# Products with stationary weights: all wide matmuls of a weight tile, then all narrow ones

## The chip, the cores and the metric

The kernel runs on one core of one Trainium2 chip. The metric is the device time of one execution in microseconds.

## What is computed

The reference is a decoder trunk of two layers on 256 tokens of width 2048, in float32: a dilated sliding-window attention (layer A), a SwiGLU feed-forward, a multi-head latent attention (layer B), a second feed-forward, each with an RMS norm ahead and a residual sum behind, and a last norm. Nearly all work is products of the tokens with weight matrices:

```python
qkv = (xn @ w_qkv).reshape(b, s, N_A_GROUPS, 3, A_HEADS, A_HEAD_DIM)   # layer A: 3 groups of q, k, v
g, u = jnp.split(xn @ w_gu, 2, axis=-1)                                # feed-forward, hidden 5632
return (jax.nn.silu(g) * u) @ w_down
kv = (c @ w_kv_b).reshape(b, s, B_HEADS, B_NOPE_DIM + B_V_DIM)         # layer B
q = (cq @ w_q_b).reshape(b, s, B_HEADS, B_NOPE_DIM + B_ROPE_DIM)
```

## The kernel before

**Weights.** Every weight matrix is read once, in tiles of up to 1 MB in the order of use (`WeightStream`, from line 83). SP loads them ahead. Each float32 tile is split into two float32r parts, `hi` and `lo`, whose sum is the weight exactly: ScalarE (ACT) casts `hi` (L141), VectorE (DVE) subtracts to get `lo` (L142), in two halves per tile. Both parts have three buffers; the split runs two weight tiles ahead of TensorE (PE), so that the split of tile n + 2 writes the buffers of tile n - 1 and waits for PE's last use of each.

**Products.** The tokens' activations are split in the same way and lie side by side in one tile, `xT[:, k, 0:256]` (hi) and `xT[:, k, 256:512]` (lo). `product` (L423) fetches weight tile after weight tile and accumulates into one PSUM tile `acc` of two banks, of which there are two. It has two forms:

- `w_stationary` (L391): 128 columns of weights stand still, the tokens stream. For each of the 8 feature tiles `kk` of a weight tile and each of its 2 column groups `i`, there is a **wide** matmul of 512 columns (`hi` on tokens hi and lo, L398) and a **narrow** one of 256 columns (`lo` on tokens hi alone, L402), both into bank `i` of `acc`. They alternate: narrow, wide, narrow, wide, with the bank changed after each pair. Only at the first feature tile of a product the wide one comes first, since it starts the accumulation. It computes q and k of layer A (1536 pairs of a wide and a narrow), gate and up of both feed-forwards (2816 pairs), and in layer B keys, queries and their rotary parts (176 pairs, in weight tiles of 4 or 8 feature tiles and 1 or 2 column groups).
- `x_stationary` (L409): 128 tokens stand still and the weights stream, three matmuls per feature tile and token tile (L419, L420, L421), each with its own stationary tile, three in a row into the same bank. They are 512 columns wide; for the values of layer B 256.

Every matmul has its own weight load (LDWEIGHTS, the rows PEld).

**After a product.** `halves` adds the two halves of `acc`: ACT copies the second (L438), DVE adds the first (L439). Then follow, on DVE and ACT, rotary embedding and masks, or SiLU and the product of gate and up. `Later` puts the work that depends on these behind the matmuls of the following weight tiles: scores of layer A two weight tiles later, values three, in layer B one and two. A scheduler orders the instructions of every engine by its own estimate of when they are ready.

Of the kernel before, what the change touches and what calls it, by code (L numbers as in the profile page):

```python
# [16 lines left out]
P = 128  # L17
S = 256
NT = S // P
# [17 lines left out]
# Weight tiles between a head's projections and its scores, its values.  # L37
# [9 lines left out]
def shape_constants():  # L47
    """Identity, attention masks and rotary tables: functions of the shapes alone."""
    c = np.zeros((P, C_END), np.float32)
    c[:, C_ID:C_ID + P] = np.eye(P, dtype=np.float32)  # L50

    def allowed(q, k, window, dil):
        dist = q - k
        return (dist >= 0) & (dist <= window) & (dist % dil == 0)

    def put(at, blocks):
        m = np.concatenate([allowed(q[:, None], k[None, :], w, d) for q, k, w, d in blocks], axis=1)
        c[:, at:at + m.shape[1]] = np.where(m, np.float32(0.0), np.float32(NEG))

    # Layer A keeps the even tokens in tile 0 and the odd ones in tile 1.  # L60
    i = np.arange(P)
    par = (2 * i, 2 * i + 1)
    order = np.concatenate(par)
    put(C_M0, [(q, order, *A_GROUPS[0]) for q in par])
    put(C_M1, [(q, q, *A_GROUPS[1]) for q in par])
    put(C_M2, [(q, q, *A_GROUPS[2]) for q in par])
    put(C_MB, [(i, i, S, 1), (i + P, np.arange(S), S, 1)])

    def angles(dim):
        f = np.float32(THETA) ** (-np.arange(0, dim, 2, dtype=np.float32) / np.float32(dim))  # L70
        a = np.arange(S, dtype=np.float32)[:, None] * f.astype(np.float32)[None, :]
        return np.cos(a).T.astype(np.float32), np.sin(a).T.astype(np.float32)

    ca, sa = (t[:, order] for t in angles(A_ROT))
    c[:A_ROT, C_CA:C_CA + S] = np.concatenate([ca, ca], axis=0)
    c[:A_ROT, C_SA:C_SA + S] = np.concatenate([-sa, sa], axis=0)
    cb, sb = angles(ROPE)
    c[:, C_CB:C_CB + S] = np.concatenate([cb, cb, cb, cb], axis=0)
    c[:, C_SB:C_SB + S] = np.concatenate([-sb, sb, -sb, sb], axis=0)
    return c  # L80


class WeightStream:
    """Weight tiles in the order of use: loads run ahead, and each float32 tile is split
    exactly into two float32r parts (hi + lo) ahead of the matmuls. form: "dup" writes the
    columns of every k twice, "heads" puts the rotary columns of a pair of heads side by side."""
# [17 lines left out]
    def pieces(self, raw, hi, lo, form, gain):  # L104
        """(source, hi, lo, gain) of every split operation."""
        _, nk, ncol = raw.shape
        if form == "heads":
            for a, b, at in ((0, NOPE, 0), (NOPE, QH, 2 * NOPE)):
                src = raw.rearrange("p k (h e) -> p k h e", h=2)[:, :, :, a:b]
                dst = [t[:, :, at:at + 2 * (b - a)].rearrange("p k (h e) -> p k h e", h=2) for t in (hi, lo)]  # L110
                for hh in range(2):
                    yield src[:, :, hh, :], dst[0][:, :, hh, :], dst[1][:, :, hh, :], None
        elif gain is None:
            flat = lambda t: t.rearrange("p k c -> p (k c)")  # noqa: E731
            n = nk // 2
            for ks in (slice(0, n), slice(n, nk)):
                yield flat(raw[:, ks]), flat(hi[:, ks]), flat(lo[:, ks]), None
        else:
            for k in range(nk):
                src, dst = raw[:, k, :], [hi[:, k, :], lo[:, k, :]]  # L120
                if form == "dup":
                    src = src.unsqueeze(1).broadcast_to([P, 2, ncol])
                    dst = [t.rearrange("p (o c) -> p o c", o=2) for t in dst]
                yield src, dst[0], dst[1], gain[:, k:k + 1]

    def split(self, upto):
        nc = self.nc
        while self.n_split < min(upto, len(self.units)):
# [8 lines left out]
            view = lambda t: t[:, :nk * ncol].rearrange("p (k c) -> p k c", c=ncol)  # noqa: E731  # L137
# [23 lines left out]
class Later:  # L161
    """Work put behind the matmuls of the following weight tiles, so that TensorE has those to do
    while the other engines prepare its operands."""
# [16 lines left out]
def kernel(ctx, tc, consts, x, attn_norm_g, ffn_norm_g, a_w_qkv, a_w_o, kv_norm_g,  # L180
# [23 lines left out]
    # TensorE's clock rises after some microseconds of work: have it up when the data is here.  # L204
# [10 lines left out]
    def gain_cols(vec, name):  # L215
        """vec [n * P] -> [P, n]: rows of P, to be turned by a transpose."""
        n = vec.shape[0] // P
        row = tmp.tile([P, 2, S], F32, tag="t1", name=name + "_row")[:n, 0, :P]
        nc.scalar.dma_start(out=row, in_=vec.rearrange("(k p) -> k p", p=P))
        cols = cpool.tile([P, n], F32, name=name)  # L220

        def turn():
            ps = bank()
            nc.tensor.transpose(out=ps[:, :n], in_=row, identity=ident[:n, :n])
            nc.vector.tensor_copy(out=cols, in_=ps[:, :n])
        return cols, turn
# [9 lines left out]
    def load_rest():  # L236
        """The constants and gains that the first products don't need."""
# [78 lines left out]
    con = lambda at, n, rows=P: cst[:rows, at - P:at - P + n]  # noqa: E731  # L316
# [6 lines left out]
    def put_split(dst_hi, dst_lo, src, scale=None):  # L323
        """dst_hi + dst_lo = src (times a value per partition), exactly."""
# [8 lines left out]
    def squares(src, total, on_vector=False):  # L333
        """total [P, 1] = the sum of squares of src [P, n] along the free axis."""
# [9 lines left out]
    def transposed(srcs, dstT, k0, gain):  # L344
        """srcs: [P tokens, n] by token tile -> dstT[:, k0 + j, hi 0:S | lo S:2S], features on partitions."""
# [16 lines left out]
    def rsqrt_mean(ssq, n, dst):  # L362
        """dst = (ssq / n + eps) ** -0.5."""
# [4 lines left out]
    def token_scale(ssq, name):  # L368
        """rms scale by token from partial sums of squares [P, NT, n]."""
# [6 lines left out]
    def across(r, name):  # L376
        """r [P tokens, NT] -> [P, S], the tokens' values along the free axis of every partition."""
# [13 lines left out]
    def w_stationary(acc, hi, lo, xT, k0, first, last, cols):  # L391
        """acc[:, i, :] += (weights' columns cols(i))^T [xT hi | xT lo], lo parts of weights on xT hi."""
        nk = hi.shape[1]
        for kk in range(nk):
            k = k0 + kk
            for i, sl in enumerate(cols):
                st, sp = first and kk == 0, last and kk == nk - 1
                big_mm = lambda: mm(out=acc[:, i, :], lhsT=sl(hi, kk), rhs=xT[:, k, :],  # noqa: B023,E731  # L398
                                    start=st, stop=sp)  # noqa: B023
                if st:  # L400
                    big_mm()
                mm(out=acc[:, i, 0:S], lhsT=sl(lo, kk), rhs=xT[:, k, 0:S], start=False, stop=False)  # L402
                if not st:
                    big_mm()
# [4 lines left out]
    def x_stationary(acc, hi, lo, xT, k0, first, last, rhs=None, ncol=512, ts=range(NT)):  # L409
        """acc[:, t, :] += (tokens of tile t) @ weights."""  # L410
# [12 lines left out]
    def product(stationary, xT, K, **kw):  # L423
        """xT's K feature tiles with the next weight tiles, into a new accumulator."""
# [10 lines left out]
    def halves(acc, n, dst):  # L435
        """dst [P, n, S] = acc[:, :, :S] + acc[:, :, S:]."""
# [4 lines left out]
    def masked(dst, ps, mk, mx):  # L441
        """dst = ps + mk, mx = its maximum by row."""
# [3 lines left out]
    def softmax(parts, m, scale, nscale):  # L446
        """parts[t] [P queries, keys] masked scores, m [P, NT] their maxima -> probabilities."""
        nb = small.tile([P, NT], F32, tag="sm_nb", name="sm_nb")
        if isinstance(scale, float):
            nc.vector.tensor_scalar(out=nb, in0=m, scalar1=nscale, scalar2=None, op0=ALU.mult)  # L450
            by = lambda t: scale  # noqa: E731
        else:
            nc.vector.tensor_tensor(out=nb, in0=m, in1=nscale, op=ALU.mult)
            by = lambda t: scale[:, t:t + 1]  # noqa: E731
# [10 lines left out]
    def keys_first(blocks):  # L465
        """Transposes of [P, P] blocks of probabilities, side by side."""
# [27 lines left out]
    with tc.tile_pool(name="attn_a", bufs=2) as ap:  # L494

        def rope_a(t):
            sw = ap.tile([A_ROT, 2, S], F32, tag="sw", name="sw", bufs=1)
            nc.vector.stream_shuffle(sw, t[:A_ROT], swap)
            bc = lambda r: r.unsqueeze(1).broadcast_to([A_ROT, 2, S])  # noqa: E731
# [22 lines left out]
        def values_a(head, sm, vs):  # L522
# [11 lines left out]
            back = lambda d: d.rearrange("p (i t) -> p t i", t=NT)  # noqa: E731  # L534
# [38 lines left out]
    def out_projection(acc, oT, gain, name):  # L573
        """h += attention output @ w_o (its first columns in acc); the next normed operand,
        still to be scaled by token, and that scale."""
# [12 lines left out]
    def ffn(xT, rstd, finish):  # L588
        """h += swiglu(xT scaled by token); finish(c, t) when a piece of h is complete."""
        row = {}  # L590
        later.put(1, lambda: row.update(R=across(rstd, "R")))
        with tc.tile_pool(name="ffn", bufs=2) as fp:
            for part, (k0, n) in enumerate(FFN_PARTS):
# [15 lines left out]
                def add(acc, c, t):  # L609
                    nc.vector.scalar_tensor_tensor(out=chunk(t, c), in0=acc[:, t, :], scalar=rstd[:, t:t + 1],  # L610
                                                   in1=chunk(t, c), op0=ALU.mult, op1=ALU.add)
                    if last:  # noqa: B023
                        finish(c, t)

                for c in range(4):
# [4 lines left out]
                    else:  # the very last columns: one token tile after the other  # L620
# [29 lines left out]
    with tc.tile_pool(name="attn_b", bufs=2) as bp:  # L650

        def rope_b(dst, t):
            """dst(rows) = rotary of t [P = 2 x (32 | 32), S]."""
# [8 lines left out]
        def latent(at, gain, lag):  # L662
            """rms_norm(xT @ (gained weights)) into ccT, transposed and gained."""
# [25 lines left out]
        # Rotary queries of one head of a pair each, zero in the other head's rows.  # L689
# [127 lines left out]
```

## Time and profile before

| | |
|---|---|
| runs | 2730.53, 2730.87, 2733.0 us; median 2730.87 us |
| span of the profiled execution, first to last instruction | 2728.2 us, 2.7 us under that median |
| PE busy | 2715.6 us (100%) |
| DVE, ACT busy | 1612.6 us (59%), 1204.2 us (44%) |
| DMA | 495.91 MB, 182 GB/s on average |

The time of the profiled execution itself is not on the page; its span is. Busy PE means that some matmul is under way, not that matmuls start as fast as they can: matmuls are pipelined and the next one starts before the record of the one ahead ends. The distance between starts is to be read from the timeline.

### The profile page before, as it was taken

To read this page: it belongs to the slowest core of one execution; us is meant where nothing else is said; L and a number is where in the kernel's file an instruction comes from. 1 tells how busy PE (TensorE), PEld (TensorE's weight loads), DVE (VectorE), ACT (ScalarE), POOL (GpSimd) and SP (SyncE) were. 2 spreads that over 40 slices of the span, in tenths; PEclk is the share of its full clock that TensorE was granted. 3 is DMA by queue.
4 is the path that set the end of the run, shared out by engine and by line. 5 is a ranking of instruction groups with operands and counts; after the bars stand their busy time and mean duration, and the time that the engine had idled before them with its cause. 6 is when DMAs were issued, how large, how long until landed. Compare 5 with 4: busy or idle time off the path is not lost.

```text
span 2728.2 us, 34772 instructions
## 1 busy us (share of the span) xinstructions
PE 2715.6 (100%) x14398; PEld 2323.1 (85%) x14398; DVE 1612.6 (59%) x2240; ACT 1204.2 (44%) x1605; POOL 5.5 (0%) x12
## 2 busy tenths in 40 slices
PE   9999999999999999999999999999999999999998
PEld 7888888888888888888888888888888888888887
DVE  5666576576477555545555555587555555555554
ACT  5344444443434444434443444555444434443443
POOL 0000000000000000000000000000000000000000
PEclk9999999999999999999999999999999999999999
DMA  7545555554554555555555555454555555555553
GB/s 282 182 162 171 181 171 170 185 182 161 182 175 166 201 181 188 187 190 194 188 185 187 185 187 196 140 156 145 174 181 186 194 190 187 187 190 192 185 201 124
DMA packets 389870, 495.91 MB, mean 182 GB/s; under 512 B 9848, under 2 KB 293200, under 8 KB 389200
## 3 DMA queue, kind: packets, MB, share of 16 engines
q1 hardware_dynamic: 389088, 492.63, 54.2%
q8 instruction: 113, 1.85, 0.3%
q10 hardware_dynamic: 624, 1.07, 0.1%
q14 instruction: 45, 0.37, 0.0%
HBM read 491.57 MB, written 2.10 MB: 181 GB/s over the span
## 4 chain that ended last, share of the span: by engine, by line
PE 98%; DVE 0%; issue 0%; ACT 0%; DMA 0%; SPq 0%; POOL 0%; POOLq 0%; DVEq 0%; ACTq 0%
PE acc L398 39%; PE acc L402 20%; PE acc L420 12%; PE acc L421 12%; PE acc L419 12%; PE bank L513 1%; PE bank L470 1%; PE bank L528 1%; PE bank L351 1%; PE bank L532 1%; PE bank L705 0%; PE bank L704 0%; PE bank L715 0%; DMA xt<-in_x_dram 0%; DVE lo L142 0%
## 5 line engine op out<-in xcount | busy, mean ns | idle before, releaser
L142 DVE TENSOR_TENSOR lo<-raw,hi 128x1024 fp32r<-128x1024 f32 (+2 forms) x930 | 1082.4, 1193 | 570.4 <-ACT hi L141 570.1
L141 ACT CAST hi<-raw 128x1024 fp32r<-128x1024 f32 (+2 forms) x930 | 912.7, 1030 | 859.7 <-issue 358.8
L398 PE MATMUL acc<-xT_f,hi 128*128 128x512 f32 x2816 | 987.6, 398 | 0.0
L402 PE MATMUL acc<-xT_f,lo 128*128 128x256 f32 x2816 | 776.9, 281 | 0.0
L398 PEld LDWEIGHTS acc<-xT_f,hi 128*128 128x128 f32 x2816 | 523.8, 188 | 122.7
L398 PE MATMUL acc<-xT_a,hi 128*128 128x512 f32 x1536 | 544.2, 399 | 0.0
L402 PEld LDWEIGHTS acc<-xT_f,lo 128*128 128x128 f32 x2816 | 531.8, 189 | 7.8
L402 PE MATMUL acc<-xT_a,lo 128*128 128x256 f32 x1536 | 423.7, 281 | 0.0
L398 PEld LDWEIGHTS acc<-xT_a,hi 128*128 128x128 f32 x1536 | 286.8, 188 | 63.5
L438 ACT COPY t<-acc 128x512 f32<-128x512 f32 x161 | 92.7, 576 | 502.8 <-PE acc L398 502.8
L402 PEld LDWEIGHTS acc<-xT_a,lo 128*128 128x128 f32 x1536 | 289.5, 188 | 3.7
L419 PE MATMUL acc<-hi,hT 128*128 128x512 f32 x704 | 274.1, 389 | 0.0
L421 PE MATMUL acc<-hi,hT 128*128 128x512 f32 x704 | 273.9, 389 | 0.0
L420 PE MATMUL acc<-lo,hT 128*128 128x512 f32 x704 | 273.9, 389 | 0.0
L439 DVE TENSOR_TENSOR gu<-acc,t 128x512 f32<-128x512 f32 x88 | 60.9, 692 | 244.2 <-ACT t L438 244.2
L421 PEld LDWEIGHTS acc<-hi,hT 128*128 128x128 f32 x704 | 132.1, 188 | 27.5
L420 PEld LDWEIGHTS acc<-lo,hT 128*128 128x128 f32 x704 | 132.1, 188 | 27.3
L419 PEld LDWEIGHTS acc<-hi,hT 128*128 128x128 f32 x704 | 132.2, 188 | 27.2
L420 PE MATMUL acc<-lo,xT_a 128*128 128x512 f32 x384 | 150.3, 391 | 0.8 <-DVE lo L142 0.8
L421 PE MATMUL acc<-hi,xT_a 128*128 128x512 f32 x384 | 151.0, 393 | 0.0
L419 PE MATMUL acc<-hi,xT_a 128*128 128x512 f32 x384 | 150.9, 393 | 0.0
L420 PEld LDWEIGHTS acc<-lo,xT_a 128*128 128x128 f32 x384 | 72.3, 188 | 16.1 <-DVE lo L142 1.5
(169 smaller groups left out, 2080.7 us busy)
## 6 DMA issues: line engine op xcount, KB each, us to landing
raw<-in_ffn_w_gu_dram SPq DMA_DIRECT2D x176, 1024.0 KB, 4.9
raw<-in_a_w_qkv_dram SPq DMA_DIRECT2D x143, 1024.0 KB, 4.9
raw<-in_ffn_w_down_dram SPq DMA_DIRECT2D x88, 1024.0 KB, 4.9
raw<-in_a_w_o_dram SPq DMA_DIRECT2D x16, 1024.0 KB, 4.9
raw<-in_b_w_o_dram SPq DMA_DIRECT2D x16, 1024.0 KB, 4.9
raw<-in_b_w_kv_b_dram SPq DMA_DIRECT2D x8, 1024.0 KB, 5.4
raw<-in_b_w_q_b_dram SPq DMA_DIRECT2D x8, 768.0 KB, 4.6
raw<-in_b_w_q_a_dram SPq DMA_DIRECT2D x4, 1024.0 KB, 5.0
```

Source lines behind the costliest of these rows:

```text
L141: nc.scalar.copy(out=h, in_=src)
L142: nc.vector.tensor_tensor(out=l, in0=src, in1=h.bitcast(F32), op=ALU.subtract)
L351: nc.tensor.transpose(out=ps[:, jj * S + t * P:jj * S + (t + 1) * P], in_=srcs[t][:, (j + jj) * P:(j + jj + 1) * P], identity=ident)
L398: big_mm = lambda: mm(out=acc[:, i, :], lhsT=sl(hi, kk), rhs=xT[:, k, :], # noqa: B023,E731 start=st, stop=sp) # noqa: B023
L402: mm(out=acc[:, i, 0:S], lhsT=sl(lo, kk), rhs=xT[:, k, 0:S], start=False, stop=False)
L419: mm(out=acc[:, t, :ncol], lhsT=xh, rhs=rhs(hi, kk), start=st, stop=False)
L420: mm(out=acc[:, t, :ncol], lhsT=xh, rhs=rhs(lo, kk), start=False, stop=False)
L421: mm(out=acc[:, t, :ncol], lhsT=xl, rhs=rhs(hi, kk), start=False, stop=sp)
L438: nc.scalar.copy(out=t1[:, :n, :], in_=acc[:, :n, S:2 * S])
L439: nc.vector.tensor_tensor(out=dst, in0=acc[:, :n, 0:S], in1=t1[:, :n, :], op=ALU.add)
L470: nc.tensor.transpose(out=ps[:, i * P:(i + 1) * P], in_=b, identity=ident)
L513: mm(out=ps[:, t * n:(t + 1) * n], lhsT=q[:, hh, qt], rhs=kt[:, hh, ks], start=True, stop=True)
```

## The change

In `w_stationary` the loops are turned round: for each weight tile first all wide matmuls (column group by column group, the 8 feature tiles of one after each other), then all narrow ones in the same order. The matmuls, their operands and their number are the same. The accumulation still starts with a wide matmul, and it now ends with a narrow one. The rest of the change takes out comments.

```diff
     def w_stationary(acc, hi, lo, xT, k0, first, last, cols):
         nk = hi.shape[1]
-        for kk in range(nk):
-            k = k0 + kk
-            for i, sl in enumerate(cols):
-                st, sp = first and kk == 0, last and kk == nk - 1
-                big_mm = lambda: mm(out=acc[:, i, :], lhsT=sl(hi, kk), rhs=xT[:, k, :],
-                                    start=st, stop=sp)
-                if st:
-                    big_mm()
-                mm(out=acc[:, i, 0:S], lhsT=sl(lo, kk), rhs=xT[:, k, 0:S], start=False, stop=False)
-                if not st:
-                    big_mm()
+        for i, sl in enumerate(cols):
+            for kk in range(nk):
+                mm(out=acc[:, i, :], lhsT=sl(hi, kk), rhs=xT[:, k0 + kk, :], start=first and kk == 0, stop=False)
+        for i, sl in enumerate(cols):
+            for kk in range(nk):
+                mm(out=acc[:, i, 0:S], lhsT=sl(lo, kk), rhs=xT[:, k0 + kk, 0:S], start=False,
+                   stop=last and kk == nk - 1)
```

On PE, in the middle of the first feed-forward (`xT_f` are its tokens), over the end of one product and the start of the next, before:

```order
L402 MATMUL acc<-xT_f_7145,lo 128x256
L398 MATMUL acc<-xT_f_7145,hi 128x512
L402 MATMUL acc<-xT_f_7145,lo 128x256
L398 MATMUL acc<-xT_f_7145,hi 128x512 x2
L402 MATMUL acc<-xT_f_7145,lo 128x256
L398 MATMUL acc<-xT_f_7145,hi 128x512
L402 MATMUL acc<-xT_f_7145,lo 128x256 x2
L398 MATMUL acc<-xT_f_7145,hi 128x512
```

and after (the lines are three fewer, so L397 is the wide one and L400 the narrow one):

```order
L397 MATMUL acc<-xT_f_7145,hi 128x512 x16
L400 MATMUL acc<-xT_f_7145,lo 128x256 x16
L397 MATMUL acc<-xT_f_7145,hi 128x512 x16
L400 MATMUL acc<-xT_f_7145,lo 128x256 x16
L397 MATMUL acc<-xT_f_7145,hi 128x512 x16
```

A weight tile is now a run of 16 wide and a run of 16 narrow matmuls.

On ACT, in the same feed-forward (`t` is the copied half of an accumulator, `gu` gate and up, `hT` their product), before:

```order
L438 COPY t_8250<-acc 128x512
L141 CAST hi<-raw 128x1024 x2
L604 ACTIVATE gu_8249<-gu_8249 128x512
L141 CAST hi<-raw 128x1024 x2
L438 COPY t_8337<-acc 128x512
L141 CAST hi<-raw 128x1024 x2
L326 CAST hT<-gu_8336 128x2x256
```

and after:

```order
L435 COPY t_8250<-acc 128x512
L141 CAST hi<-raw 128x1024
L601 ACTIVATE gu_8249<-gu_8249 128x512
L141 CAST hi<-raw 128x1024 x3
L435 COPY t_8337<-acc 128x512
L141 CAST hi<-raw 128x1024
L326 CAST hT<-gu_8336 128x2x256
```

One cast of the coming weight tiles has moved ahead of each copy out of an accumulator, and one behind it is left. In layer B the same happens to the second copy of a pair of heads (the rotary queries), in six of the eight pairs; before and after:

```order
L438 COPY t_14260<-acc 128x512
L438 COPY t_14264<-acc 128x256
L141 CAST hi<-raw 128x1024 x2
L326 CAST oT_b<-bank 128x256
L472 COPY pt<-bank 128x384
```

```order
L435 COPY t_14260<-acc 128x512
L141 CAST hi<-raw 128x1024
L435 COPY t_14264<-acc 128x256
L141 CAST hi<-raw 128x1024
L326 CAST oT_b<-bank 128x256
```

The second copy stands behind one half of a cast. DVE's order in layer B is unchanged; in the feed-forward and in layer A a half of the `lo` split stands ahead of later steps of a product's chain.

## Rows read from the trace of the kernel before

**Rows 1.** The page: busy time, granted clock, chain, groups (busy us, mean ns).

```profile
PE 2715.6 (100%) x14398; PEld 2323.1 (85%) x14398; DVE 1612.6 (59%) x2240; ACT 1204.2 (44%) x1605; POOL 5.5 (0%) x12
...
PEclk9999999999999999999999999999999999999999
...
PE 98%; DVE 0%; issue 0%; ACT 0%; DMA 0%; SPq 0%; POOL 0%; POOLq 0%; DVEq 0%; ACTq 0%
PE acc L398 39%; PE acc L402 20%; PE acc L420 12%; PE acc L421 12%; PE acc L419 12%; PE bank L513 1%; PE bank L470 1%; PE bank L528 1%; PE bank L351 1%; PE bank L532 1%; PE bank L705 0%; PE bank L704 0%; PE bank L715 0%; DMA xt<-in_x_dram 0%; DVE lo L142 0%
...
L142 DVE TENSOR_TENSOR lo<-raw,hi 128x1024 fp32r<-128x1024 f32 (+2 forms) x930 | 1082.4, 1193 | 570.4 <-ACT hi L141 570.1
L141 ACT CAST hi<-raw 128x1024 fp32r<-128x1024 f32 (+2 forms) x930 | 912.7, 1030 | 859.7 <-issue 358.8
L398 PE MATMUL acc<-xT_f,hi 128*128 128x512 f32 x2816 | 987.6, 398 | 0.0
...
L398 PE MATMUL acc<-xT_a,hi 128*128 128x512 f32 x1536 | 544.2, 399 | 0.0
```

**Rows 2.** Windows, narrow line L402, feed-forward: window, length, PE busy (count), PEld, clock, DMA.

```profile
1248.83:1429.41 180.58, 141.18 (x512) 96.70 (x512) 1.00 0.57 187
```

**Rows 3.** Timeline, feed-forward, a border of products: start us, length us, engine, line.

```profile
1303.61 0.40 PE L398 MATMUL acc<-xT_f,hi 128*128 128x512 f32 x1
1303.85 0.28 PE L402 MATMUL acc<-xT_f,lo 128*128 128x256 f32 x1
1303.85 0.19 PEld L398 LDWEIGHTS acc<-xT_f,hi 128*128 128x128 f32 x1
1303.97 0.40 PE L398 MATMUL acc<-xT_f,hi 128*128 128x512 f32 x1
...
1304.67 0.40 PE L398 MATMUL acc<-xT_f,hi 128*128 128x512 f32 x1
...
1305.03 0.62 PE L398 MATMUL acc<-xT_f,hi 128*128 128x512 f32 x2
...
1305.46 0.59 ACT L438 COPY t<-acc 128x512 f32<-128x512 f32 x1 [3.61 <-PE acc L398]
1305.49 0.28 PE L402 MATMUL acc<-xT_f,lo 128*128 128x256 f32 x1
...
1305.84 0.40 PE L402 MATMUL acc<-xT_f,lo 128*128 128x256 f32 x2
...
1306.07 0.40 PE L398 MATMUL acc<-xT_f,hi 128*128 128x512 f32 x1
...
1306.08 0.69 DVE L439 TENSOR_TENSOR gu<-acc,t 128x512 f32<-128x512 f32 x1 [2.79 <-ACT t L438]
```

**Rows 4.** Timeline, PE, second product of the feed-forward: first and last of 99 rows.

```profile
1169.72 0.39 PE L421 MATMUL acc<-hi,hT 128*128 128x512 f32 x1
...
1191.94 0.39 PE L420 MATMUL acc<-lo,hT 128*128 128x512 f32 x1
```

**Rows 5.** Timeline, PE, values of layer B: first and last of 24 rows.

```profile
1775.93 0.28 PE L419 MATMUL acc<-hi,ccT 128*128 128x256 f32 x1
...
1778.69 0.28 PE L421 MATMUL acc<-hi,ccT 128*128 128x256 f32 x1
```

**Rows 6.** Windows, L402, uninterrupted stretches of layer A: first, third, last of 24, sum.

```profile
81.62:114.08 32.46, 25.50 (x92) 17.37 (x92) 1.00 0.55 182
...
141.08:161.54 20.46, 16.28 (x59) 11.11 (x59) 1.00 0.48 159
...
873.62:882.98 9.36, 7.48 (x27) 5.07 (x27) 1.00 0.39 126
sum 461.50, PE 364.68 PEld 248.69; mean PE 15.19 PEld 10.36
```

**Rows 7.** Window, layer B's heads, all engines: length, busy of PE, PEld, DVE, ACT.

```profile
1770.00:1890.00 120.00, 119.05 (x751) 106.47 (x750) 104.52 (x281) 73.24 (x168) 0.00 (x0) 1.00 0.46 145
```

**Rows 8.** PE's waits, the longest for an accumulator: total us, times, longest.

```profile
PE acc L398 <- ACT vb L731: 0.7, 1, 0.7
```

## The prediction

> **What bounds the kernel now.** I read the page first: TensorE (PE) is busy over the whole span, its granted clock is full in every slice, and the chain that ended last is 98% PE; 59% of it lies on the two lines that the change touches, L398 (wide) and L402 (narrow) [rows 1]. DVE and ACT, which make the weights' parts, are busy 59% and 44%. So the time is the number of matmuls times the distance from the start of one to the start of the next. The duration of a record is no use for that: a wide's record lasts 398 ns [rows 1], but the next matmul starts well before its end, as the timeline shows [rows 3]. I therefore took distances between starts from timelines and windows.
>
> In the feed-forward part, 512 narrows (and as many wides) fill 180.58 us [rows 2]: 352.7 ns per pair. The timeline shows its pattern: wide 1303.61, narrow 1303.85, wide 1303.97, and the wide three pairs after the first at 1304.67, so 1.06 us for three pairs [rows 3]; a wide takes about 236 ns to the next start and a narrow 117 ns. In layer A the same loop runs at more than one pace: 32.46 us for 92 pairs (352.8 ns), but 20.46 us for 59 (346.8 ns). All 24 uninterrupted stretches together, of which the first, the third, the last and the sum stand in the rows, hold 4 x 330 = 1320 pairs (the four groups of heads repeat one pattern of counts) in 461.50 us: 349.6 ns [rows 6].
>
> **What the new order costs, from the nearest rows.** No long run of wides or of narrows of this function is in the trace, but x_stationary has both, with a new stationary tile for every matmul as here.
> - Wide after wide: the first and the last of 99 rows of the feed-forward's second product start at 1169.72 and 1191.94 us [rows 4]: 22.22/98 = 226.7 ns. The function itself does it once, where one product ends and the next begins: two wides from 1305.03 to the narrow at 1305.49, 0.46 us [rows 3]; with 0.227 for the second, the one after a narrow keeps its 0.235.
> - Narrow after narrow: in layer B 24 narrow matmuls in a row start from 1775.93 to 1778.69 us [rows 5]: 2.76/23 = 120.0 ns. The function does it once per product: two narrows from 1305.84 to the wide at 1306.07, 0.23 us [rows 3], which leaves some 115 ns for the one behind a wide.
>
> So what counts is what stood ahead: a wide is 9 ns cheaper behind a wide, a narrow 5 ns dearer behind a narrow.
>
> A weight tile of 8 feature tiles and 2 column groups is now 16 wides, then 16 narrows: 235 + 15 x 226.7 + 115 + 15 x 120.0 = 5550 ns, or 346.9 per pair. That the fastest stretch of the alternating loop also runs at 346.8 [rows 6] suggests that this is the floor of both orders, which the alternation reaches only at times.
>
> **The sum.**
> - Feed-forward, 2816 pairs [rows 1]: 352.7 - 346.9 = 5.8 ns each, 16.3 us.
> - Layer A, 1536 pairs [rows 1]: 349.6 - 346.9 = 2.7 ns each, 4.1 us.
> - Layer B, 176 pairs, 4 to 8 at a time: at the same 2.7 ns 0.5 us. Against it stands a moved instruction: in six of eight pairs of heads half a cast of weights now stands ahead of ACT's second copy out of an accumulator. Such a cast takes 1.03 us on average [rows 1], so at most 6.2 us if all reached PE, and nothing if the next scores have that much slack. PE stands idle for 0.95 of 120 us there, with DVE at 87% [rows 7]. I take these two as cancelling: 0.
>
> Together 20.4 us off. The profiled execution's span is 2728.2 us; the median of the runs is 2730.9, with 2.7 us around the span. Off the median: **2710.5 us**.
>
> **Edits that I cost at nothing.** The instructions are the same in kind and number, the scores and values go to the same products, and PE still waits twice per weight tile for ACT's parts and twice for DVE's. The last wide now frees the hi tile some 1.9 us before the weight tile ends (16 x 0.12), so the cast two tiles ahead begins earlier and stands ahead of ACT's copy of the accumulator; two halves of 1.03 us [rows 1] end some 0.2 us after the product. On DVE a half of the next split (1.19 us [rows 1]) stands ahead of the addition that empties the accumulator, the rest of the product's chain behind it. Today the copy starts at 1305.46 us with the product's end and DVE's addition at 1306.08 [rows 3]; both would come 1 to 2 us later. The accumulator is wanted again one product later, some 11 us, which hides it; the scores of layer A run two weight tiles, 11 us, behind their product, and the wait for lo is looser than before, since lo is used last. If that cover went, PE would lose those 1 to 2 us per product. The longest wait of PE for an accumulator is 0.7 us today, and it comes once [rows 8].
>
> **Rivals.**
> 1. *The order does not matter: no change.* A wide costs 236 and a narrow 117 ns in this loop because of its operands (tokens stream, weights stand), whatever stands ahead. For it: the two kinds of loop differ in what streams, and the wide that follows a narrow at a border of products costs the same as within. Against: the second of two wides at that border comes out at 227, if the first keeps its 235, as in x_stationary. The sum is then 0: 2731 us. The Trainium skill has a rule to this effect (TensorE: Matmul & The Clock Gate, Back-to-back issue gap): an isolated matmul's distance is its columns divided by 2.4 GHz plus 2.5 ns, so 216 and 109 ns, 325 a pair in any order, and no gain here. The trace disagrees with its size: no order comes below 346 ns, and 120.0 in a run stands against 109.
> 2. *A run of narrows waits for its weights: slower.* A weight load is recorded with 0.19 us, more than a narrow's 120 ns [rows 3, 5], and with wides between, only every other load has so short a slot. If in this loop a load were shown in full, a narrow in a run would go to 188 ns: 4230 of them (15 of 16 on 272 weight tiles, 150 in layer B) x 68 = 288 us; halfway 144 us, so 2855 us. It costs more than the order brings from about 125 ns per narrow on, 5 ns above the rows. Against it: layer B's run of 24, with a load each, holds 120.0 ns throughout. The Trainium skill puts a load at its columns divided by 1.2 GHz, 107 ns for 128 (same page, LDWEIGHTS (loading the stationary operand)), as long as a narrow streams; by that the loads would fit, as that run shows.
> 3. *Half of the wides' gain is had.* Wides at 231 ns behind each other: 15 x 4.3 ns given back on each of 272 weight tiles, 17.5 us, so 2728 us. It counts with rival 1.
> 4. *Narrows stay at 115 ns behind each other:* 15 x 5 ns x 272 = 20.4 us more gain, 2690 us. The run in layer B is against it.
> 5. *The change does not do what it says.* The built order shows rows of 16 and 16, broken only by scores and values of layer A, so this I leave out.
>
> **How the numbers follow.** Chances: the forecast 0.82; rivals 1 and 3 together 0.10, of which 0.08 end within 0.2%; rival 2, 0.05; rival 4, 0.03. Within 0.2% is 5.5 us either way, about what a measurement of this kernel can tell from no change. The forecast itself reaches from 2702 (narrows in a run keep 2 of the 5 ns, 8 us) to 2723 (wides keep 1.6 ns of their 9, 6.5 us, and layer B's moved casts cost their 6 us). That leaves out rival 4 below and rivals 1 to 3 above, some 0.18. Faster: 0.82 + 0.03 + 0.02 = 0.87; same 0.08; slower 0.05.
>
> **What would show it.** In the profile after: the timeline of a weight tile with wides 0.227 us apart and narrows 0.120; the 512 pairs of the feed-forward window in some 177.6 us; layer A's stretches all at 347 ns; PE's idle in layer B near 1 us; the granted clock still full. Narrows of 125 ns and more mean rival 2, wides of 235 ns rival 1. Waits of PE for accumulators, or for scores' operands, would mean that the moved casts and copies reach it. The prediction is wrong if the distances depend on the operands and not on what stood ahead.

## The result and the profile after

The changed kernel takes 2714.7 us (median of five runs, 2713.9 to 2715.6) against 2731.5 us for the kernel before on the same chip (median of five, 2730.5 to 2733.0): a ratio of 0.9939, with a 95% interval from 0.9927 to 0.9951, 16.8 us off. Timed again beside the experiments it came to 2715.7 us against 2730.1, 0.9947 [0.9933, 0.9961]. So it is faster, by 0.6% where 0.75% was forecast: 4.2 us above the forecast of 2710.5 us, within the stated range of 2702 to 2723 us.

The page of the changed kernel, the lines that answer to [rows 1]. L397 is now the wide line and L400 the narrow one:

```profile
span 2713.6 us, 34687 instructions
...
PE 2698.9 (99%) x14398; PEld 2327.4 (86%) x14398; DVE 1607.1 (59%) x2240; ACT 1205.5 (44%) x1605; POOL 5.5 (0%) x12
...
PEclk9999999999999999999999999999999999999999
...
PE 98%; DVE 1%; ACT 0%; issue 0%; DMA 0%; SPq 0%; POOL 0%; POOLq 0%; DVEq 0%; ACTq 0%
...
L397 PE MATMUL acc<-xT_f,hi 128*128 128x512 f32 x2816 | 672.0, 391 | 0.0
...
L400 PE MATMUL acc<-xT_f,lo 128*128 128x256 f32 x2816 | 365.3, 283 | 0.0
```

PE still bounds the kernel, at full granted clock, with the same number of matmuls. The busy time of L397 has fallen by 316 us against L398 before, and that says nothing: a line's busy time counts every moment in which one of its records runs. Before, a wide and a narrow record overlapped and both lines counted that time; in a run, records of the same line overlap and it is counted once. The distances between starts tell what moved. First the window over the same 512 pairs as [rows 2], narrow line; then, on the timeline, the runs of 16 (start, length to the end of the last, count):

```profile
1244.82:1422.92 178.10, 66.25 (x512) 65.64 (x512) 1.00 0.58 191
```

```profile
1265.14 2.08 PE L400 MATMUL acc<-xT_f,lo 128*128 128x256 f32 x16
1267.06 3.82 PE L397 MATMUL acc<-xT_f,hi 128*128 128x512 f32 x16
1270.71 2.08 PE L400 MATMUL acc<-xT_f,lo 128*128 128x256 f32 x16
1272.62 1.55 PE L397 MATMUL acc<-xT_f,hi 128*128 128x512 f32 x6
```

178.10 us for 512 pairs is 347.9 ns a pair; it was 352.7. A run of 16 narrows takes 1.92 us from its first start to that of the next run, a run of 16 wides 3.65 us. That is 228 ns per wide, not 226.7, and the timeline shows which wides it is. This is the same run, cut behind its sixth wide:

```profile
1266.94 0.28 PE L400 MATMUL acc<-xT_f,lo 128*128 128x256 f32 x1
1267.06 1.55 PE L397 MATMUL acc<-xT_f,hi 128*128 128x512 f32 x6
```

The sixth ends 1.55 us behind the start of the first and is 0.39 us long, so it starts 1.16 us behind it: five distances of 232 ns. In the trace they are 233, 236, 228, 233 and 231 ns, to within a nanosecond the same five in every run of wides of the feed-forwards that stands behind narrows; from the sixth on all are 226 or 227, and the remaining eleven make up 2.49 of the 3.65 us. Behind x_stationary, whose matmuls are 512 columns wide too, there are no slow wides, in layer A and in the feed-forwards alike. Here is the first run of layer A:

```profile
81.17 0.39 PE L418 MATMUL acc<-hi,xT_a 128*128 128x512 f32 x1
81.39 3.79 PE L397 MATMUL acc<-xT_a,hi 128*128 128x512 f32 x16
85.02 2.08 PE L400 MATMUL acc<-xT_a,lo 128*128 128x256 f32 x16
```

From 81.39 to 85.02 are 3.63 us, 226.9 ns per wide.

Where the time went, by the start of each stage's first matmul on the two timelines (us):

| stage | before | after | off | forecast off |
|---|---|---|---|---|
| up to the first q, k product | 80.61 | 81.39 | -0.8 | 0 |
| layer A, from there to its output projection | 802.75 | 800.37 | 2.4 | 4.1 |
| first feed-forward | 740.00 | 733.29 | 6.7 | 8.15 |
| second feed-forward, to the end | 745.54 | 738.85 | 6.7 | 8.15 |
| layer B and both output projections | 359.33 | 359.67 | -0.3 | 0 |

That is 14.7 us between the two profiled spans; the medians, of five executions each, are 16.8 us apart. In the first line the second part of the tokens landed later in the profile after: PE's transposition of it starts at 8.79 us, not at 8.05. None of the matmuls that the change reorders stands ahead of it, and over all profiles of this case the line lies between 80.3 and 82.1 us.

### The profile page after: what moved, and what is told of

Read it like the earlier page. It is cut to its first block, busy times and chain, and to the rows that moved or that the text cites. A ratio compares the mean times of both kernels' runs of the same rounds, so it can differ in the third digit from the quotient of the medians.

```text
span 2713.6 us, 34687 instructions
## 1 busy us (share of the span) xinstructions
PE 2698.9 (99%) x14398; PEld 2327.4 (86%) x14398; DVE 1607.1 (59%) x2240; ACT 1205.5 (44%) x1605; POOL 5.5 (0%) x12
## 4 chain that ended last, share of the span: by engine, by line
PE 98%; DVE 1%; ACT 0%; issue 0%; DMA 0%; SPq 0%; POOL 0%; POOLq 0%; DVEq 0%; ACTq 0%
PE acc L397 38%; PE acc L400 20%; PE acc L417 12%; PE acc L418 12%; PE acc L416 12%; PE bank L510 1%; PE bank L467 1%; PE bank L525 1%; PE bank L351 1%; PE bank L529 1%; PE bank L702 0%; PE bank L701 0%; PE bank L712 0%; DVE lo L142 0%; DMA xt<-in_x_dram 0%
## 5 line engine op out<-in xcount | busy, mean ns | idle before, releaser
L397 PE MATMUL acc<-xT_f,hi 128*128 128x512 f32 x2816 | 672.0, 391 | 0.0
L397 PEld LDWEIGHTS acc<-xT_f,hi 128*128 128x128 f32 x2816 | 517.8, 188 | 100.8 <-DVE xT_f L330 0.3
L397 PE MATMUL acc<-xT_a,hi 128*128 128x512 f32 x1536 | 379.4, 395 | 0.0
L400 PEld LDWEIGHTS acc<-xT_f,lo 128*128 128x128 f32 x2816 | 361.0, 191 | 13.7
L400 PE MATMUL acc<-xT_f,lo 128*128 128x256 f32 x2816 | 365.3, 283 | 0.0
L397 PEld LDWEIGHTS acc<-xT_a,hi 128*128 128x128 f32 x1536 | 281.5, 188 | 53.9
L400 PEld LDWEIGHTS acc<-xT_a,lo 128*128 128x128 f32 x1536 | 196.9, 191 | 7.5
L400 PE MATMUL acc<-xT_a,lo 128*128 128x256 f32 x1536 | 199.2, 283 | 0.0
L418 PEld LDWEIGHTS acc<-hi,xT_a 128*128 128x128 f32 x384 | 72.3, 188 | 14.8
```

The source lines that it names most:

```text
L397: mm(out=acc[:, i, :], lhsT=sl(hi, kk), rhs=xT[:, k0 + kk, :], start=first and kk == 0, stop=False)
L400: mm(out=acc[:, i, 0:S], lhsT=sl(lo, kk), rhs=xT[:, k0 + kk, 0:S], start=False, stop=last and kk == nk - 1)
L418: mm(out=acc[:, t, :ncol], lhsT=xl, rhs=rhs(hi, kk), start=False, stop=sp)
```

## The experiments

Times without a range are of one run. Each diff is against the changed kernel and shows only the lines that matter; lines taken out are mostly left out. The kernels are read by the window of the second gate-and-up part of the first feed-forward, 512 pairs, as in [rows 2]. Two theories stood at the start: that only the matmul just ahead counts (*neighbour*, the one on record in the prediction), and that every change from narrow to wide costs five slow wides (*change*). Two rivals: that staying in one PSUM bank brought the gain (*banks*), and that PE's waits for the weights' parts make the slow wides (*waits*).

### Two wides, two narrows

```diff
+        for kk in range(nk):
+            for i, sl in enumerate(cols):
+                mm(out=acc[:, i, :], lhsT=sl(hi, kk), rhs=xT[:, k0 + kk, :], start=first and kk == 0, stop=False)
+            for i, sl in enumerate(cols):
+                mm(out=acc[:, i, 0:S], lhsT=sl(lo, kk), rhs=xT[:, k0 + kk, 0:S], start=False,
+                   stop=last and kk == nk - 1)
```

> For each feature tile two wides (one per column group), then two narrows. Read in the window of the feed-forward's second gate-and-up part, 512 pairs; there the kernel before took 352.7 ns per pair and the changed one 347.85. Theory 'neighbour' (only the matmul just ahead counts: wide after narrow 235, wide after wide 227, narrow after wide 115, narrow after narrow 120): (235+227+115+120)/2 = 348.5 ns, so about 12 us off the time of before. Theory 'change' (after a narrow the next five wides are slow, 233, 236, 228, 233, 231, the first narrow after wides takes 113): two wides 233+236, two narrows 113+119, 350.5 ns, 6 us off. Theory 'banks' (the gain comes from staying in one PSUM bank): bank changes at every matmul, so no gain, 352 ns or more.

Measured: 2715.9 us. The window (narrow line L399) and the timeline:

```profile
1244.45:1422.79 178.34, 100.42 (x512) 96.18 (x512) 1.00 0.57 189
```

```profile
1260.46 0.63 PE L397 MATMUL acc<-xT_f,hi 128*128 128x512 f32 x2
1260.93 0.39 PE L399 MATMUL acc<-xT_f,lo 128*128 128x256 f32 x2
1261.16 0.62 PE L397 MATMUL acc<-xT_f,hi 128*128 128x512 f32 x2
```

348.3 ns per pair: almost the total that *neighbour* expects, 348.5, and by the wrong parts. Two wides take 0.47 us and two narrows 0.23 us; in the trace the four wides of a period are 233, 236, 233 and 231 ns and the narrows 116, 112, 113 and 119. A wide behind a wide takes 236 or 231 ns where 227 was expected, and a narrow behind a narrow 112 or 119 where 120 was. The misses nearly cancel. So the rule of the prediction is wrong, and *change* in its first form, which expected 350.5, is wrong here too: every second pair of wides takes 464 ns, not 469, and every second pair of narrows 228, not 232.

### Eight wides, eight narrows

```diff
+        for i, sl in enumerate(cols):
+            for kk in range(nk):
+                mm(out=acc[:, i, :], lhsT=sl(hi, kk), rhs=xT[:, k0 + kk, :], start=first and kk == 0, stop=False)
+            for kk in range(nk):
+                mm(out=acc[:, i, 0:S], lhsT=sl(lo, kk), rhs=xT[:, k0 + kk, 0:S], start=False,
+                   stop=last and kk == nk - 1)
```

> Column group by column group: 8 wides, then 8 narrows, so twice as many changes from narrow to wide as in the changed kernel. 'Neighbour': a change costs 8-5 = 3 ns, so per 8 pairs 8x346.7+3: 347.1 ns per pair. 'Change': a change costs 27 ns on five wides less 7 on one narrow, 20 ns, per 8 pairs: 8x346.7+20 = 2794, 349.2 ns per pair, some 5 us slower than the changed kernel. 'Banks' (each run stays in one bank): no more than the changed kernel, 347.8 or less.

Measured: 2720.7 us, 5 to 6 us slower than the changed kernel.

```profile
1246.98:1425.73 178.75, 71.23 (x512) 69.85 (x512) 1.00 0.58 190
```

349.1 ns per pair: *change* had 349.2, *neighbour* 347.1, and by *banks* it could not be above 347.8. Per eight pairs it is 8 x (349.1 - 346.7) = 19 ns above the floor, with the same five slow wides.

### Every second weight tile turned round, and the changed kernel beside it

```diff
+        for run in (wide, narrow) if first else (narrow, wide):
+            run()
```

`wide` and `narrow` are the two loops of the change, with the end of the accumulation at whichever comes last. A product of two weight tiles now runs 16 wides, 32 narrows, 16 wides, and the next product begins with wides.

> Every second weight tile of a product in the reverse order, narrows first: runs of 32 wides and 32 narrows, so half as many changes from narrow to wide in layer A and the feed-forwards. 'Change': 20 ns saved on 136 of the 272 weight tiles, 2.7 us under the changed kernel (2712 us against 2714.7); 346.7+20/32 = 347.3 ns per pair in the feed-forward window. 'Neighbour': 3 ns on 136, 0.4 us, no difference to be seen. Theory 'waits' (the slow wides are those at the start of a weight tile, where PE waits twice for ACT's casts): the wides at the start of every weight tile stay slow, also behind wides; 347.85 ns as before.

> The changed kernel once more beside the others, for the comparison with the turned order: 2714.7 us, 347.85 ns per pair in the feed-forward window, five slow wides (233, 236, 228, 233, 231 ns) behind every run of narrows. All theories expect the same here.

Measured: 2711.9 us (five runs, 2711.8 to 2712.9), ratio to before 0.9934 [0.9921, 0.9946]; the changed kernel beside it 2715.7 us (2715.4 to 2716.0), five runs too, which do not overlap. The turned order is 3.9 us faster by the medians, 3.1 us by the two profiled spans (2710.5 and 2713.6); *change* had 2.7. Window and timeline of the turned kernel:

```profile
1243.06:1420.88 177.82, 63.93 (x512) 63.54 (x512) 1.00 0.58 192
```

```profile
1261.63 7.44 PE L398 MATMUL acc<-xT_f,hi 128*128 128x512 f32 x32
1268.92 4.00 PE L404 MATMUL acc<-xT_f,lo 128*128 128x256 f32 x32
1272.75 7.44 PE L398 MATMUL acc<-xT_f,hi 128*128 128x512 f32 x32
```

347.3 ns per pair, as *change* has it. Half of the weight tiles begin with wides behind wides, and those are 227 ns from the first on although they depend on ACT's casts in the same way: that speaks against *waits*. By the stages of the table above, the two feed-forwards are together 1.5 us shorter than in the changed kernel beside it (20 ns on 88 weight tiles would be 1.8), and layer A is 1.4 us shorter (on 48, 1.0). This version beats both kernels.

### The bank and the grouping, one without the other

All wides first, feature tile by feature tile, so that the bank changes with every matmul:

```diff
+        for kk in range(nk):
+            for i, sl in enumerate(cols):
+                mm(out=acc[:, i, :], lhsT=sl(hi, kk), rhs=xT[:, k0 + kk, :], start=first and kk == 0, stop=False)
+        for kk in range(nk):
+            for i, sl in enumerate(cols):
+                mm(out=acc[:, i, 0:S], lhsT=sl(lo, kk), rhs=xT[:, k0 + kk, 0:S], start=False,
+                   stop=last and kk == nk - 1)
```

> All wides of a weight tile first, as in the changed kernel, but feature tile by feature tile, so that the PSUM bank changes with every matmul instead of every eighth. The change does two things at once, it groups the wides and it stays in one bank for eight matmuls; this keeps the first alone. Theory 'change' (a run of narrows makes the five wides behind it slow, 20 ns a time; all else at 226.7 and 120): 347.85 ns per pair in the feed-forward window, 2715 us. Theory 'banks': the gain is gone, 352 to 353 ns, 2730 us.

Measured: 2715.5 us, and the window gives 347.9 ns:

```profile
1245.18:1423.28 178.10, 66.25 (x512) 65.64 (x512) 1.00 0.58 191
```

The reverse, wide and narrow in turn but 16 matmuls in a row in one bank:

```diff
+        for i, sl in enumerate(cols):
+            for kk in range(nk):
+                mm(out=acc[:, i, :], lhsT=sl(hi, kk), rhs=xT[:, k0 + kk, :], start=first and kk == 0, stop=False)
+                mm(out=acc[:, i, 0:S], lhsT=sl(lo, kk), rhs=xT[:, k0 + kk, 0:S], start=False,
+                   stop=last and kk == nk - 1)
```

> Wide and narrow alternate as before, but column group by column group, so that 16 matmuls in a row write one bank: the other half of the change alone. 'Banks': most of the gain, 347 to 348 ns per pair in the feed-forward window. 'Change': 352.7 as before, or another of the paces that the alternation already shows in layer A (346.8, 349.8, 352.8), since what it locks to depends on what stood ahead; so the median somewhere from 2712 to 2731 us with, in each product, one of these three paces.

Measured: 2734.1 us, where before ran 2732.3 beside it:

```profile
1250.35:1431.23 180.88, 143.67 (x512) 96.74 (x512) 1.00 0.57 186
```

353.3 ns per pair, and both numbers are a little above what *change* allowed (352.8 ns at most, 2731 us). The grouping alone has the whole gain, the bank none.

### One cast for a weight tile

```diff
-            n = nk // 2
-            for ks in (slice(0, n), slice(n, nk)):
+            for ks in (slice(0, nk),):
```

> Each weight tile without gains is split in one cast and one subtraction instead of two halves, so PE waits once for hi and once for lo per weight tile, not twice; the order of the changed kernel else. Theory 'waits' (wides 1 to 5 are slow because the first and the fifth wait for ACT): the slowness ends with the first wide or two, 346.9 to 347.3 ns per pair. Theories 'change' and 'lead': the same five slow wides, 347.85 ns.

Measured: 2718.8 us; the window:

```profile
1246.85:1424.96 178.11, 66.26 (x512) 65.64 (x512) 1.00 0.58 192
```

347.9 ns, with the same five slow wides. *Waits* is out. The span is 3.5 us longer than that of the changed kernel, and none of it lies in this window: by the stages 1.6 us lie in layer A, 1.1 in layer B and the output projections, 0.9 in the rest of the feed-forwards. Which waits make them I did not follow.

### Other widths of the narrow matmuls

By now *change* left open what it is that changes: the weights' part, their buffers, the load's room, or the streamed length. First 384 columns:

```diff
-                mm(out=acc[:, i, 0:S], lhsT=sl(lo, kk), rhs=xT[:, k0 + kk, 0:S], start=False,
+                mm(out=acc[:, i, 0:3 * P], lhsT=sl(lo, kk), rhs=xT[:, k0 + kk, 0:3 * P], start=False,
```

> The changed kernel with the narrow matmuls 384 columns wide instead of 256 (lo times half of the tokens' lo part is added too, which the kernel leaves out). By 13.3 ns above the streamed columns, as 226.7 is above 512/2.4 and 120.0 above 256/2.4, such a run should go at 173.3 ns, so 400.0 ns per pair without any cost of a change. Theory 'lead' (a run of narrows goes at the pace of its weight loads, the loads lose their lead over the matmuls, and five wides pay for winning it back): a load fits well into 173 ns, so no slow wides behind the run, 400.0 ns per pair in the feed-forward window. Theory 'change' without regard to width: wides at 233, 236, 228, 233, 231 again, 401.2 ns.

Measured: 2967.8 us; window and timeline:

```profile
1360.24:1567.13 206.89, 94.56 (x512) 90.47 (x512) 1.00 0.50 166
```

```profile
1373.13 3.83 PE L397 MATMUL acc<-xT_f,hi 128*128 128x512 f32 x16
1376.80 2.96 PE L400 MATMUL acc<-xT_f,lo 128*128 128x384 f32 x16
1379.60 3.83 PE L397 MATMUL acc<-xT_f,hi 128*128 128x512 f32 x16
```

404.1 ns, above both expectations. A run of wides takes 3.67 us (16 x 226.7 = 3.63) and a run of the others 2.80 us (16 x 173.3 = 2.77): now both directions pay. In the trace nine wides settle, 229, 233, 236, 224, 231, 236, 228, 233, 231, and behind them the others start at 171, 175, 177, 185, 176, 182 before they stay at 173 or 174. A load has room in 173 ns: in the run with 128 columns below, load and matmul together keep a pace of 112 ns. So *lead* falls.

Then 512 columns, the same length as the wides:

```diff
+                mm(out=acc[:, i, 0:2 * S], lhsT=sl(lo, kk), rhs=xT[:, k0 + kk, 0:2 * S], start=False,
```

> The changed kernel with the narrow matmuls as wide as the wide ones, 512 columns (lo times both parts of the tokens, which the kernel leaves out for the second). Theory 'length' (it is the change of the streamed length that costs, in both directions: the run with 384 columns had slow matmuls behind both changes): nothing changes its length any more, so every distance is 226.7 ns from the first on, 453.3 ns per pair in the feed-forward window. Theory 'kind' (it is the change from lo to hi, other tiles, other buffers, PE's waits at the start of a run): some five slow wides behind every run of lo, 27 ns per weight tile, 455 ns per pair.

Measured: 3190.6 us; window and timeline:

```profile
1460.54:1692.65 232.11, 121.09 (x512) 96.11 (x512) 1.00 0.45 149
```

```profile
1482.30 3.79 PE L397 MATMUL acc<-xT_f,hi 128*128 128x512 f32 x16
1485.93 3.79 PE L400 MATMUL acc<-xT_f,lo 128*128 128x512 f32 x16
1489.55 3.79 PE L397 MATMUL acc<-xT_f,hi 128*128 128x512 f32 x16
```

453.3 ns, every run 3.63 us, no slow wide anywhere in the window. The order, the waits, the weights' parts and the loads are those of the changed kernel; only the length no longer changes. So the cost belongs to the change of the streamed length.

And 128 columns:

```diff
+                mm(out=acc[:, i, 0:P], lhsT=sl(lo, kk), rhs=xT[:, k0 + kk, 0:P], start=False,
```

> The changed kernel with the narrow matmuls 128 columns wide (lo times the second half of the tokens is left out). If the streamed columns set the pace, 128/2.4+13.3 = 66.7 ns in a run; if the weight load sets it, which is recorded with 188 to 192 ns at any width, the distance stays near 120. Theory 'loads bind' (rival 2 of the prediction in a mild form: at 256 columns load and stream are about equal): 107 to 120 ns per narrow, 335 to 347 ns per pair. Otherwise about 294 ns per pair. Theory 'length': slow wides behind the run as with 256 columns or worse, 20 to 40 ns per weight tile.

Measured: 2700.6 us; window and timeline:

```profile
1239.59:1414.62 175.03, 60.56 (x512) 62.03 (x512) 1.00 0.58 194
```

```profile
1261.37 3.90 PE L397 MATMUL acc<-xT_f,hi 128*128 128x512 f32 x16
1265.11 1.90 PE L400 MATMUL acc<-xT_f,lo 128*128 128x128 f32 x16
1266.85 3.90 PE L397 MATMUL acc<-xT_f,hi 128*128 128x512 f32 x16
```

341.9 ns. Half the columns of the narrows save 6 ns a pair: behind the first (57 ns) the distances are 109 to 115 ns, 112 on average, where the streamed columns would allow 67. So something else sets the pace here. The weight load is the likely one, as *loads bind* had it; no run takes the loads away to show it. The Trainium skill (TensorE: Matmul & The Clock Gate, LDWEIGHTS (loading the stationary operand)) puts a load at its columns divided by 1.2 GHz, an estimate of 107 ns for 128 columns of weights; the run's 112 ns are within 5 ns of it. If it is the load, rival 2 of the prediction is true of 128 columns and not of 256.

The wides are slow here too, by more than the 20 to 40 ns per weight tile that *length* had: 292 ns for the first, then 235, 233, 236, 224, 231, 236, 228, 233 and 231 before they stay at 226 or 227. A run takes 3739 ns, 112 above 16 x 226.7. About half of that comes back at the other end, where the first narrow takes 57 ns in place of 112.

## Why the prediction was right, and where not

- **What bounds the kernel, and what the time is made of**: right. PE at full clock, number of matmuls times distance; its idle time stayed small. Layer B's window after, against [rows 7], has PE busy for 118.46 of 120 us, 0.6 less, and that stage and the output projections lost 0.3 us:

```profile
1761.70:1881.70 120.00, 118.46 (x750) 105.50 (x750) 103.99 (x281) 74.05 (x168) 0.00 (x0) 1.00 0.46 145
```

- **The two paces in long runs**, 226.7 and 120.0 ns from x_stationary [rows 4, 5]: right to the nanosecond in w_stationary as well. That what streams or stands decides (rival 1) is refuted, as are loads binding at 256 columns (rival 2), wides at 231 ns (rival 3; the mean in a run is 228.4) and narrows staying at 115 ns (rival 4).
- **The change between the runs**: the mis-sized term. The working took 235 + 115 for the first wide and the first narrow, 3 ns above 226.7 + 120.0, from a border of products where a single pair of wides stands (in nanoseconds 236 and 227 for those wides, 117 and 121 for the narrows). Measured, the first two narrows take 113 and 119 ns, 8 below two of 120, and the five wides 233, 236, 228, 233, 231, 28 above five of 226.7, so 20 ns. With 16 x 346.7 + 20 = 5567 ns per weight tile, or 347.9 a pair, the sum becomes 2816 x 4.8 = 13.5 us for the feed-forwards and 1536 x 1.7 = 2.6 us for layer A; the stages show 13.4 and 2.4, where 16.3 and 4.1 were forecast.
- **The range**: it held in part by luck. Its upper end allowed for wides that keep 1.6 ns of their 9, which comes close to the 1.7 ns by which the mean wide lies above 226.7; but it was meant as a small excess of every wide, and the runs show it on the first five alone, set off by a change of length that the working took to cost 3 ns.
- **The sentence that went too far**: "what counts is what stood ahead". Two wides and two narrows in turn show that a matmul's distance depends on more than the one ahead, and so do the two orders side by side: the second wide at the border of products before takes 227 ns, the second wide of a run after 236, and both stand behind one wide that stands behind a narrow. It takes five wides here, nine at 384 columns and ten at 128, to settle behind a change of length. Alternation does not settle in these traces: the 353 ns before is a lasting unsettled pace (241, 120, 236, 113, 233, 117 ns, over and over), and layer A's stretches at 346.8 [rows 6] are another that alternation can fall into. Those were read rightly as the floor: no order of a 512 and a 256 went below 346.7 over a longer stretch.
- **Layer A's paces gone**: right; its stretches of whole weight tiles between scores and values run at 347.9 ns, to within the rounding of the windows. Here are the first of 20, with 64 pairs, and the sum of all, with 704 (line L397):

```profile
86.93:109.20 22.27, 15.27 (x65) 11.77 (x65) 1.00 0.61 203
...
sum 244.91, PE 167.93 PEld 129.34; mean PE 8.40 PEld 6.47
```

- **The moved casts and copies** at nothing: right. The longest wait of PE for an accumulator is still the one of [rows 8]:

```profile
PE acc L397 <- ACT vb L728: 0.7, 1, 0.7
```

  What has grown is the waiting of the scores' weight loads in layer A for `mx`, DVE's step that masks the scores before and takes their maximum (total us, times, longest). It cost little: layer A fell short of its sum by 0.2 us, and in the turned kernel, where these waits are 2.2 us again, layer A gained 0.4 us more than the changes of length explain. Before and after:

```profile
PEld bank L513 <- DVE mx L443: 2.2, 8, 0.3
```

```profile
PEld bank L510 <- DVE mx L440: 5.4, 20, 0.5
```

What stays open is the mechanism in the engine. The runs show that the streamed length and its history decide, not bank, waits, buffers, the part of the weights, or (with 384 columns) the load's room; why wides settle over just this series was not found.

## What to carry to other kernels

On an engine that is always busy, measure the distance from start to start, by shape and by what stands ahead; the records' lengths don't tell it. Where matmuls of two lengths alternate, group them in runs as long as buffers and accumulation allow, and turn every second group round so that equal lengths meet at the borders: here that brought 0.5 to 0.6% for the grouping and 3 to 4 us more for the turning. Longer isn't better at every step: the window gave 353 ns a pair for runs of one, 348.3 for two, 349.1 for eight, 347.9 for 16 and 347.3 for 32, so measure the run length that you mean to use. A pace taken from a long run elsewhere carries over; the cost of a border must be taken from a border between runs of that length.

## What the runs showed of the hardware

With new weights for every matmul, float32r matmuls in runs of one length start every 226.7 ns (512 columns), 173.3 (384) and 120.0 (256): 128 columns more cost 53.3 ns, which is 2.4 columns per ns at full granted clock, and 13.3 ns are left over in each case. At 128 columns it is 112 ns, likely set by the weight load. A change of length costs extra over several matmuls, also where both lengths leave room for the load: from 384 to 512 columns nine wides, 0.04 us in all, from 512 to 384 six matmuls. The slow wides end alike: behind 384 and behind 128 columns the last eight are 233, 236, 224, 231, 236, 228, 233 and 231 ns, and behind 256 the last four are the same 236, 228, 233 and 231; what that says of the engine is open. Run by run it is the same series to within a nanosecond. Per change from 256 to 512 and back the pairs' pace above 346.7 ns comes to 19 to 20 ns with runs of 8, 16 and 32, but to some 3 ns with runs of two.
